# A second pair of gate columns by seven products a block, low parts of five weight tiles by ScalarE and adding transfers, partial sums laid back into PSUM, in a fp32 decoder layer

## The chip, the cores and the metric

One core of a Trainium2 chip. The metric is the device time of one execution in microseconds, lower is better: the median of 3 runs, 1174.49 us (1174.16 to 1174.79). Everything is fp32 in and out. TensorE (PE) multiplies, VectorE (DVE) and ScalarE (ACT) work on tiles in SBUF and PSUM, SyncE (SP) issues plain DMA transfers, GpSimd (POOL) issues the transfers that add to what lies in their target.

## What is computed

One layer over 272 tokens (16 learned ones and 256 of the input) of width 2048. The first half, in which the change lies:

```python
u = rms_norm(h, g_pre_mix[l])
proj = u @ w_in[l]                     # 2048 x 7168: z | v | g | gate_a | gate_b
z_pool, v_conv, g_conv, gate_a, gate_b = jnp.split(proj, splits, axis=-1)
y_a = causal_multiscale_pool(z_pool, w_pool_grp[l], pool_scale[l]) @ w_pool_out[l]
y_b = conformer_conv(v_conv, g_conv, w_dw[l], b_dw[l],
                     conv_ln_g[l], conv_ln_b[l]) @ w_conv_out[l]
m = jax.nn.sigmoid(gate_a) * y_a + jax.nn.sigmoid(gate_b) * y_b
h = h + rms_norm(m @ w_o[l], g_post_mix[l])
```

conformer_conv ends with a LayerNorm over the channels and a silu. The second half, an MLP of width 8192 with a squared ReLU, begins near 490 us of the profile and is the same in both kernels.

## The kernel before

**Products in three parts.** fp32 accuracy is made of fast fp32r products: every operand is split into a rounded part hi and a rest lo, and a product is hi x hi + hi x lo + lo x hi. A weight tile is 1 MB, 128 partitions x 2048. It goes through three steps: SP loads it into a *room* (a raw buffer, L821), ACT casts it to hi (L845), DVE subtracts to get lo (L851). There are three hi and three lo buffers in turn, so the cast of tile n+2 may start no sooner than the product of tile n-1 has ended. Rooms come free as stages end; `loads` (L808) takes the next weight as soon as a room is free for long enough.

**Stages.** Products 0 to 21 are the tiles of w_in for z, v and g (below: Z; 48 matmuls each, L544), product 22 the four matrices of the pooling groups (grp). Beside them DVE does the 31-tap convolution (L981). Then follows an order written out by hand, `MAIN` (L37): p is w_pool_out, a and b are the two gate zones of w_in, c is w_conv_out, o is w_o. A word like `b22` is the weight tile of column block 2 and row block kc 2, in two block products (one for each half of the tokens, t = 0 and 1) of twelve matmuls (L1281). lnm and lnv are the sums for LayerNorm's mean and variance on PE (L1124, L1154), followed on DVE and ACT by the factor, the activations of conv_out with their low part (`s_act`, L1182) and the sums of blocks of them (`forms_c`, L1209). T, CD, OF, fu, k0r, um8, h1 turn, sum or store activations.

**Seven products in place of eight.** `b0P1` to `b0P7` are a 2 x 2 x 2 block: two halves of the tokens, two row blocks, two column blocks (0 and 1). Eight block products become seven, each a sum of activation blocks (a *form*, `forms_u`) with a sum of weight tiles. The products 2, 3 and 4 are the last of their results. After 1, 5, 6 and 7 the bank holds a partial sum that a later product needs in another bank as well: the *give* (`Pair.give`, L1318) copies it out by ACT (L1330), or subtracts it by DVE for 7. `Pair.close` (L1297) adds what was given to the finished bank by DVE (L1303, L1305). The weight sums of products 5, 6, 7 and 4 are made in the room of the first tile: by DVE (L863) where the table `SUMMED` (L44) names the product, otherwise by an adding transfer from POOL (a *bring*, L867). Before, a0, a2, b0, c2 and o0 are such pairs; b's columns 2 and 3 are plain.

**What sets the order.** `Plan` (L48) collects all work of the Z and MAIN stages with its engine and what it reads and writes, gives every piece a time by which it is due (from the row of PE's products, backwards), and writes each engine's instructions in the order in which a list schedule starts them. PE keeps the order of the table. Each engine then runs its own row strictly in order.

Of the kernel before, what the change touches and what calls it, by code (L numbers as in the profile page):

```python
# [18 lines left out]
CW = 512  # L19
# [15 lines left out]
AFTER_G0 = [("z", 0), ("z", 1), ("v", 1), ("z", 2), ("g", 1), ("v", 2), ("g", 2), ("z", 3),  # L35
            ("v", 3), ("g", 3)]
MAIN = (  # L37
# [5 lines left out]
)  # L43
# [168 lines left out]
def hybrid_block(ctx: ExitStack, tc: tile.TileContext, ins: dict, out: bass.AP):  # L212
# [548 lines left out]
    for s in steps:  # L761
        if s[0] == "close":
            index_of[s[1]] = n
        if s[0] == "k1":
            index_of[10] = n
# [6 lines left out]
    index_of[8] = index_of[9] = len(products) - 2  # L772
    uses = []
    for m_, s in enumerate(products):
        if m_ == 0:
            continue
        if s[0] == "S" and s[3] in ADDS:
            onto, what = raw_of(s), block_raw(s, ADDS[s[3]])
            if s[3] in SUMMED.get((s[1], s[2]), "56"):
                uses.append((m_, "sum", [onto, what], None))  # L780
            else:
                uses.append((m_, "bring", [onto], what))
        uses.append((m_, "split", [raw_of(s)], None))
    last_use, to_load = {}, []
    for n, (m_, _, raws_, _) in enumerate(uses):
        for r in raws_:
            if r not in last_use:
                to_load.append(r)
            last_use[r] = n

    rooms = {}
    for r in range(3):
# [12 lines left out]
    early = [2]  # L805
    room_at = {}

    def loads():  # L808
        while to_load:
            r = to_load[0]  # L810
            ends_ = uses[last_use[r]][0]
# [5 lines left out]
            free_rooms.remove(q)  # L817
            src, (rows, _) = source(r)
# [18 lines left out]
    def split_of(m_, q, rows):  # L837
        box, n = split_at[m_], slot0 + m_
        width = CK * CW // (2 if m_ == 1 else 1)
        cuts = [slice(c, c + width) for c in range(0, CK * CW, width)]  # L840

        def high():
            box["flat"] = part_tile("hi", n)
            for cs in cuts:
                nc.scalar.copy(box["flat"][:, cs], rooms[q]()[:, cs])  # L845
            box["hi"] = box["flat"].rearrange("p (k c) -> p k c", k=rows)

        def low():
            lo = part_tile("lo", n)
            for cs in cuts:  # L850
                nc.vector.tensor_sub(lo[:, cs], rooms[q]()[:, cs], f32(box["flat"][:, cs]))  # L851
            box["lo"] = lo.rearrange("p (k c) -> p k c", k=rows)
        return high, low

    def weights(m_):
        while done_uses[0] < len(uses) and uses[done_uses[0]][0] <= m_:
# [8 lines left out]
            elif what == "bring":  # L865
                src, (rows, _) = source(extra)
                plan.add("POOL", 5.38, lambda a=at_rooms[0], src=src, rows=rows: nc.gpsimd.dma_start(  # L867
                    rooms[a]().rearrange("p (k c) -> p k c", k=rows), src, accum_op=ALU.add),
                    reads=names, writes=names)
            else:  # L870
                high, low = split_of(w, at_rooms[0], source(raws_[0])[1][0])
                h_, l_ = half_names(w)
                plan.add("ACT", 1.82, high, reads=names, writes=(h_,), late=0.13)
                plan.add("DVE", 2.22, low, reads=names + [h_], writes=(l_,), late=0.13)
            for r in raws_:
                if last_use[r] == n:
                    free_rooms.append(room_at[r])
# [359 lines left out]
    def finish(stage, t, n, name, src):  # L1237
# [17 lines left out]
        else:  # L1255
# [2 lines left out]
            on_vector(CW, lambda: last_factor(dst(), src(), n), (name, "gmix", dst_name),  # L1258
                      (dst_name,))

    class Pair:


        def __init__(self, stage, n0, whole):
            self.stage, self.n0, self.whole = stage, n0, whole
            self.bank = {}
            self.parts = 1 + (("N", stage, n0 + 1, 2) in products)
            self.gives = {}

        def product(self, t, n, m_, a_, names, gives, last):  # L1270
            key = (t, n)
            opens = key not in self.bank
            if opens:
                self.bank[key] = open_bank()
            bank, ends_ = self.bank[key], bool(gives or last)

            def f():
                box = split_at[m_]
                for k in range(CK):
                    for i, (part, w_) in enumerate(((0, "hi"), (0, "lo"), (1, "hi"))):  # L1280
# [2 lines left out]
                                         stop=ends_ and k == CK - 1 and i == 2,  # L1283
                                         skip_group_check=True)
            on_tensor(2.725, f, half_names(m_) + names, (bank,))
            if gives:
                gives(bank)
            if last:
# [29 lines left out]
        def give(self, s, bank):  # L1318
# [3 lines left out]
                return  # L1322
            t, j = {"1": (0, 0), "5": (1, 1), "6": (0, 1), "7": (1, 1)}[s]
            name, dst = self.place(t, n + j)
            if s == "7":
                on_vector(CW, lambda: nc.vector.tensor_sub(dst(), dst(), banks[bank]),
                          (bank, name), (name,))
# [18 lines left out]
    def counted(stage, t, n):  # L1346
        remaining[stage, t, n] -= 1
        return remaining[stage, t, n] == 0

    def product_n(m_, stage, n, kc):  # L1350
# [12 lines left out]
    def product_s(m_, stage, n0, s, k0):  # L1363
# [10 lines left out]
        row, j = INTO[s]  # L1374
        pair.product(row, n0 + j, m_, a_, waits, (lambda bank: pair.give(s, bank)) if s in "1567"
                     else None, s in "234" and counted(stage, row, n0 + j))

# [53 lines left out]
        loads()  # L1431

    def k1_step():
        free_rooms.remove(10)
        plan.take(names_s[1], ["raw10"])
        plan.take(["raw3", "raw4"], names_y)
        free_rooms.extend((4, 3))
        loads()
# [125 lines left out]
    for s in steps:  # L1564
# [29 lines left out]
        else:  # L1594
            for w in range(m_, min(m_ + 3, len(products))):
                weights(w)
            if m_ >= tail:
                break
            {"Z": product_z, "grp": product_grp, "N": product_n, "S": product_s}[s[0]](m_, *s[1:])
            m_ += 1  # L1600
    for t in range(NT):
# [751 lines left out]
```

## Time and profile before

| | |
|---|---|
| median of 3 runs | 1174.49 us (1174.16 to 1174.79) |
| the profiled execution, its own time | 1174.95 us |
| its span, first to last instruction | 1173.2 us |
| granted TensorE clock | 0.998 |
| moved by DMA | 290.07 MB, mean 247 GB/s |

The profile's first part gives the busy time of each engine with its share of the span; part four follows the chain of work that ended last. PEld is PE's loading of weights, which overlaps its matmuls. A matmul of 128x512 is listed with 0.39 us, yet the next starts 0.23 us later: matmuls are pipelined, and the distance from start to start is what one costs. In rows of a source line the three numbers of a duration are minimum, median and maximum in ns. "DMA to landing" counts from the issue.

### The profile page before, as it was taken

How to read it: one execution, taken by the hardware profiler on the slowest of the kernel's cores; microseconds unless marked ns; L12 is line 12 of the kernel's file. 1: busy time of each engine (PE TensorE's matmuls, PEld its weight loads, DVE VectorE, ACT ScalarE, POOL GpSimd, SP SyncE). 2: the span in 40 equal slices, each digit the busy share in tenths (PEclk: the TensorE clock that was granted, in tenths of full speed). 3: DMA queues.
4: the chain of work that ended last, by engine and by line, in shares of the span. 5: the costliest groups of instructions: out<-in, count | busy, mean ns of one | idle time of the engine just before them, and what ended most of it. 6: DMA issues, size and time to landing. Idle time of an engine off the chain costs nothing.

```text
span 1173.2 us, 15824 instructions
## 1 busy us (share of the span) xinstructions
PE 1161.4 (99%) x6289; PEld 1008.4 (86%) x6289; DVE 1078.6 (92%) x1169; ACT 717.9 (61%) x727; POOL 69.1 (6%) x72
## 2 busy tenths in 40 slices
PE   9999999999999999999999999999999999999997
PEld 8999998788888888898888888888888888888886
DVE  6799999999998998788998998998999989989998
ACT  6634454556478666576775665665656655656655
POOL 1000000000000000000101001000000001010000
PEclk9999999999999999999999999999999999999999
DMA  9955356889866799468999999999999998999955
GB/s 294 285 189 180 108 180 173 248 271 299 218 195 246 209 352 296 150 215 288 261 311 232 248 310 258 243 303 236 282 293 227 327 250 237 329 252 250 327 140 179
DMA packets 188194, 290.07 MB, mean 247 GB/s; under 512 B 4969, under 2 KB 94761, under 8 KB 187336
## 3 DMA queue, kind: packets, MB, share of 16 engines
q1 hardware_dynamic: 161832, 234.31, 58.3%
q0 software_dynamic: 25680, 54.03, 25.2%
q8 instruction: 49, 0.80, 0.3%
q10 hardware_dynamic: 608, 0.73, 0.2%
q14 instruction: 25, 0.20, 0.0%
HBM read 284.85 MB, written 4.19 MB: 246 GB/s over the span
## 4 chain that ended last, share of the span: by engine, by line
PE 98%; DVE 0%; DMA 0%; ACT 0%; issue 0%; ACTq 0%; DVEq 0%
PE bank_u L549 19%; PE bank_k L1281 18%; PE acc_up L2024 13%; PE acc_v L1281 10%; PE bank_u L555 9%; PE bank_k L544 8%; PE bank_a L2024 7%; PE bank_b L2024 6%; PE acc_v L544 4%; PE acc_up L549 1%; PE acc_up L555 1%; PE acc_v L1551 0%; PE bank_k L1551 0%; DMA raw<-in_w_in_dram 0%; PE ht L1616 0%; PE bank_y L1385 0%
## 5 line engine op out<-in xcount | busy, mean ns | idle before, releaser
L549 PE MATMUL bank_u<-m,hi 128*128 128x512 f32 x960 | 329.6, 390 | 0.0
L555 PE MATMUL bank_u<-m,lo 128*128 128x256 f32 x960 | 265.4, 276 | 0.0
L549 PEld LDWEIGHTS bank_u<-m,hi 128*128 128x128 f32 x960 | 180.2, 188 | 37.8
L845 ACT CAST hi<-raw_p 128x2048 fp32r<-128x2048 f32 x70 | 133.8, 1913 | 103.7 <-PE bank_k L1281 28.8
L1854 DVE TENSOR_TENSOR lo<-raw_m,hi 128x2048 fp32r<-128x2048 f32 x79 | 180.8, 2288 | 17.0 <-ACT hi L1849 16.1
L1849 ACT CAST hi<-raw_m 128x2048 fp32r<-128x2048 f32 x79 | 151.1, 1913 | 68.0 <-PE bank_u L549 48.1
L555 PEld LDWEIGHTS bank_u<-m,lo 128*128 128x128 f32 x960 | 180.3, 188 | 1.6
L851 DVE TENSOR_TENSOR lo<-raw_p,hi 128x2048 fp32r<-128x2048 f32 x70 | 159.6, 2284 | 12.7 <-ACT hi L845 12.4
L2024 PE MATMUL acc_up<-hi,forms 128*128 128x512 f32 (+1 forms) x456 | 146.9, 386 | 0.0
L1849 ACT CAST hi<-raw_h 128x2048 fp32r<-128x2048 f32 x42 | 80.3, 1912 | 38.5 <-PE bank_u L549 18.3
L2024 PEld LDWEIGHTS acc_up<-hi,forms 128*128 128x128 f32 x456 | 85.2, 188 | 18.1 <-ACT G L2049 0.2
L1854 DVE TENSOR_TENSOR lo<-raw_h,hi 128x2048 fp32r<-128x2048 f32 x42 | 96.1, 2287 | 5.1 <-ACT hi L1849 4.6
L981 DVE SCALAR_TENSOR_TENSOR c<-a,taps,c 128x256 f32<-128x256 f32 x240 | 100.1, 475 | 0.0
L544 PE MATMUL bank_k<-u_um,hi 128*128 128x272 f32 x512 | 95.2, 287 | 0.0
L1281 PE MATMUL bank_k<-hi,u_um 128*128 128x512 f32 x280 | 88.8, 389 | 0.7 <-ACT sg L1330 0.7
L2024 PE MATMUL acc_up<-lo,forms 128*128 128x512 f32 (+1 forms) x228 | 88.2, 387 | 0.0
L2024 PE MATMUL bank_a<-hi,forms 128*128 128x512 f32 x256 | 84.1, 389 | 0.0
L544 PEld LDWEIGHTS bank_k<-u_um,hi 128*128 128x128 f32 x512 | 79.8, 188 | 0.0
L544 PE MATMUL bank_k<-u_um,lo 128*128 128x272 f32 x256 | 73.3, 287 | 0.0
L1849 ACT CAST hi<-raw_c 128x2048 fp32r<-128x2048 f32 x23 | 43.9, 1908 | 39.1 <-PE bank_u L549 31.5
L2024 PE MATMUL bank_b<-hi,forms 128*128 128x512 f32 x192 | 63.1, 389 | 0.0
L1281 PEld LDWEIGHTS bank_k<-hi,u_um 128*128 128x128 f32 x280 | 52.5, 188 | 12.0 <-ACT sg L1330 1.1
(408 smaller groups left out, 2231.3 us busy)
## 6 DMA issues: line engine op xcount, KB each, us to landing
raw_p<-in_w_in_dram SPq DMA_DIRECT2D x30, 1024.0 KB, 5.6
raw_m<-in_w_down_dram SPq DMA_DIRECT2D x26, 1024.0 KB, 8.7
raw_m<-in_w_down_dram POOLq DMA_DIRECT2D x23, 1024.0 KB, 10.7
raw_h<-in_w_up_dram SPq DMA_DIRECT2D x18, 1024.0 KB, 8.1
raw_h<-in_w_down_dram SPq DMA_DIRECT2D x18, 1024.0 KB, 8.8
raw_m<-in_w_up_dram SPq DMA_DIRECT2D x17, 1024.0 KB, 8.0
raw_k<-in_w_in_dram SPq DMA_DIRECT2D x14, 1024.0 KB, 7.0
raw_a<-in_w_up_dram SPq DMA_DIRECT2D x14, 1024.0 KB, 9.1
```

Of the source, the lines that this page charges most:

```text
L544: nc.tensor.matmul(acc, w[:, k[0], cs], act[:, k[1], a, off:], start=first and n == 0, stop=last and n == 2)
L549: nc.tensor.matmul(acc.rearrange("p (a t) -> p a t", a=2)[:, :, ts], hi[:, k[0], cs], act[:, k[1], :, off + ts.start:off + ts.stop], start ...
L555: nc.tensor.matmul(acc[:, :T], lo[:, k[0], cs], act[:, k[1], 0, off:], start=False, stop=stop, skip_group_check=True)
L845: nc.scalar.copy(box["flat"][:, cs], rooms[q]()[:, cs])
L851: nc.vector.tensor_sub(lo[:, cs], rooms[q]()[:, cs], f32(box["flat"][:, cs]))
L981: nc.vector.scalar_tensor_tensor(C_c()[:, q, :], A_a()[:, q, i:i + T], taps[:, q, i:i + 1], C_c()[:, q, :], op0=ALU.mult, op1=ALU.add)
L1281: nc.tensor.matmul(banks[bank], a_(k, part), box[w_][:, k, :], start=opens and k == 0 and i == 0, stop=ends_ and k == CK - 1 and i == 2, s ...
L1849: nc.scalar.copy(box["flat"], raw_in(room))
L1854: nc.vector.tensor_sub(lo, raw_in(room), f32(box["flat"]))
L2024: nc.tensor.matmul(acc, forms[h][:, f, k, a_, :], box[w_][:, k, cs], start=start and k == 0 and n == 0, stop=stop and k == KH - 1 and n == ...
```

## The change

Five parts, all in the mix stage:

1. Columns 2 and 3 of the second gate, row blocks 0 and 1 (`b20 b21 b30 b31`), become `b2P1` to `b2P7`. `MAIN` is written anew around them, and `SUMMED` divides the sums between DVE and POOL anew.
2. `LOW_BY_DMA` names five early tiles (13, 14, 16, 18 of Z and 22, the pooling groups) whose low part isn't made by DVE: ACT writes the negated rounded tile into another room (L823), an adding transfer of POOL adds the raw weight from memory to it (L827), and ACT copies the result to lo (L883).
3. `LAY_BEHIND`: where a bank opens two products or more behind the give that its result needs, ACT copies the partial sum into the bank (`lay`, L1314), and the matmuls add to it; DVE's addition at the end is left out.
4. A plain product right behind a give into a bank that it uses itself begins with its other half of the tokens (`given`).
5. Room 10 is ready for weights at the first gate product rather than at k1.

```diff
-    "p20 p30 p01 p21 p00 p11 fu p10 p31 k1 a0P1 a2P1 a2P2 a0P5 a13 a12 a0P6 a0P3 a0P7 a02 a0P4 "
-    "a2P5 a03 a32 a33 a2P6 a2P3 a2P7 a22 a2P4 a0P2 b0P1 a23 b22 b21 b33 b23 b0P5 b32 lnm b0P6 b20 "
-    "b0P7 b31 lnv b0P4 b12 b0P3 k0r b02 b13 b0P2 b30 b03 um8 c01 c2P1 c11 c10 T10 c2P5 c2P6 c2P3 "
...
+    "p00 fu p31 p01 a0P1 p30 p21 p20 p10 p11 k1 a2P2 a0P5 a13 a0P6 a0P3 a2P1 a0P7 a12 a0P4 "
+    "a2P5 a33 a03 a2P6 a32 a2P7 a02 a2P4 a0P2 a2P3 a23 a22 b2P1 b2P5 b33 b2P2 b2P6 b2P3 b2P7 "
+    "b0P1 b23 b2P4 b32 b0P5 b0P2 lnm b22 b12 b0P6 b0P3 lnv b0P7 b02 b0P4 b03 b13 k0r um8 c2P1 "
+    "c00 c2P5 c11 c01 c10 T00 T01 c2P2 c2P6 T10 c2P3 c2P7 o20 c2P4 T11 CD o31 T21 T30 o30 T20 "
+    "T31 o21 o22 OF o0P1 o0P5 h1 o23 o0P3 o0P6 o12 o0P7 o02 o13 o0P4 o03 o0P2 o32 o33 "
-SUMMED = {('gate0', 0): '67', ('gate0', 2): '57', ('gate1', 0): '6', ('co', 2): '456', ('o', 0): '67'}
+SUMMED = {('gate0', 0): '67', ('gate0', 2): '56', ('gate1', 0): '5', ('co', 2): '6', ('o', 0): '57', ('gate1', 2): '56'}
+LOW_BY_DMA = "13 14 16 18 22"
+LAY_BEHIND = 2
...
+    def low_by_dma(m_, q):
+        low_at[m_] = q
+        raw = raw_of(products[m_])
+        src, (rows, _) = source(raw)
+
+        def minus_high(a=room_at[raw]):
+            nc.scalar.activation(rooms[q]().bitcast(F32R), rooms[a](), AF.Copy, scale=-1.0)
+
+        def add_raw():
+            whole = rooms[q]().rearrange("p (k c) -> p k c", k=rows)
+            nc.gpsimd.dma_start(whole, src, accum_op=ALU.add)
...
-            for cs in cuts:
+            for cs in cuts if m_ not in low_at else ():
                 nc.vector.tensor_sub(lo[:, cs], rooms[q]()[:, cs], f32(box["flat"][:, cs]))
+            if m_ in low_at:
+                nc.scalar.copy(lo, rooms[low_at[m_]]())
...
+        def lay(self, t, n, bank):
+
+            name, dst = self.place(t, n)
+            self.laid.add((t, n))
+            on_scalar(CW, lambda: nc.scalar.copy(banks[bank], dst()), (name,), (bank,))
...
             if opens:
                 self.bank[key] = open_bank()
+                if made[0] - self.held.get(key, made[0]) >= LAY_BEHIND:
+                    self.lay(t, n, self.bank[key])
             bank, ends_ = self.bank[key], bool(gives or last)
+            opens = opens and key not in self.laid
...
-            if self.whole or (t, n) == (1, self.n0):
+            if self.whole or (t, n) == (1, self.n0) or (t, n) in self.laid:
                 finish(self.stage, t, n, bank, src)
...
-        order_ = range(NT)
+        order_ = reversed(range(NT)) if given == [(stage, 0, n)] else range(NT)
+        given.clear()
```

**PE where a0P5 is followed by a13.** Names behind the arrow are weight part and activations; `u_um` is the first slice of a row block and `u_um_156` the other three, `forms_u` the sum for product 5; `bank_k_...` and `acc_v_...` are PSUM banks. Before:

```order
L1281 MATMUL bank_k_400<-lo_2268,forms_u 128x512
L1281 MATMUL bank_k_400<-hi_2249,forms_u 128x512
L1281 MATMUL bank_k_400<-hi_2270,u_um 128x512
L1281 MATMUL bank_k_400<-lo_2273,u_um 128x512
...
L1281 MATMUL bank_k_401<-hi_2270,u_um 128x512
L1281 MATMUL bank_k_401<-lo_2273,u_um 128x512
```

and with the change:

```order
L1330 MATMUL acc_v_1_165<-lo_2259,forms_u 128x512
L1330 MATMUL acc_v_1_165<-hi_2238,forms_u 128x512
L1330 MATMUL bank_k_399<-hi_2278,u_um 128x512
L1330 MATMUL bank_k_399<-lo_2283,u_um 128x512
...
L1330 MATMUL acc_v_1_165<-hi_2278,u_um 128x512
L1330 MATMUL acc_v_1_165<-lo_2283,u_um 128x512
```

a13 went on in the bank that a0P5 had just filled and that is copied out at this point; now its twelve matmuls for the other half of the tokens stand in between, in a bank of their own.

**ACT in the Z stage, tiles 15 to 18**, with the change. hi_1308, hi_1372, hi_1437 and hi_1502 are the casts of tiles 15, 16, 17 and 18; the two L823 are the negated copies of 16 and 18, lo_1443 the low part of 16.

```order
L875 CAST hi_1308<-raw_s0a 128x2048
L823 ACTIVATE raw_p_405<-raw_p_406 128x2048
L823 ACTIVATE raw_s0a<-raw_p_407 128x2048
L875 CAST hi_1372<-raw_p_406 128x2048
L875 CAST hi_1437<-raw_s0a 128x2048
L883 CAST lo_1443<-raw_p_405 128x2048
L1004 ACTIVATE g_666<-g_666 128x272
L875 CAST hi_1502<-raw_p_407 128x2048
```

Before, the four casts follow each other with nothing but convolution work between; now the negated copies stand right behind tile 15's cast, and the low part of tile 16 is read on ACT behind the cast of tile 17, in the place of a subtraction on DVE.

**ACT in the gate stage around b0P2**, with the change. hi_2964, hi_3000, hi_3019, hi_3050 and hi_3073 are the casts of b32, b0P5, b0P2, b22 and b12, which is the order of the products; `sg_2088` holds the partial sums and acc_v_0_164 is the bank of b0P2.

```order
L875 CAST hi_2964<-raw_p_405 128x2048
L1382 COPY sg_2088<-bank_k_402 128x512
L875 CAST hi_3000<-raw_p_406 128x2048
L875 CAST hi_3019<-raw_k_2276 128x2048
L875 CAST hi_3050<-raw_k_2276 128x2048
L1314 COPY acc_v_0_164<-sg_2088 128x512
L1277 ACTIVATE sg_2088<-sg_2088,r_in 128x512
L875 CAST hi_3073<-raw_p_405 128x2048
```

The L1314 copy, which b0P2's matmuls wait for, stands behind the cast of b22, the product after b0P2; before there was no such copy, and DVE added the partial sum after the bank was finished.

More of the change, by code (lines that the diff above doesn't have):

```diff
@@ L772, in hybrid_block @@
     index_of[8] = index_of[9] = len(products) - 2
+    first_gate = index_of[10] = next(m_ for m_, s in enumerate(products)
+                                     if s[0] in "NS" and s[1][:4] == "gate")
     uses = []
@@ L789, in hybrid_block @@
             last_use[r] = n
+        if what == "split" and m_ in lows:
+            to_load.append(("lo", m_))
     rooms = {}
@@ L806, in hybrid_block @@
     room_at = {}
+    low_at, planned = {}, set()
+    def low_by_dma(m_, q):
[7 more added lines that the diff above has]
+            nc.gpsimd.dma_start(whole, src, accum_op=ALU.add)
+        plan.add("ACT", 1.82, minus_high, reads=(f"raw{room_at[raw]}",), writes=(f"raw{q}",),
+                 late=0.13)
+        plan.add("POOL", 5.38, add_raw, reads=(f"raw{q}",), writes=(f"raw{q}",))
     def loads():
@@ L870, in weights @@
             else:
+                planned.add(w)
                 high, low = split_of(w, at_rooms[0], source(raws_[0])[1][0])
@@ L873, in weights @@
                 plan.add("ACT", 1.82, high, reads=names, writes=(h_,), late=0.13)
-                plan.add("DVE", 2.22, low, reads=names + [h_], writes=(l_,), late=0.13)
+                if w in low_at:
+                    plan.add("ACT", 1.82, low, reads=(f"raw{low_at[w]}",), writes=(l_,), late=0.13)
+                    free_rooms.append(low_at[w])
+                else:
+                    plan.add("DVE", 2.22, low, reads=names + [h_], writes=(l_,), late=0.13)
             for r in raws_:
@@ L1259, in finish @@
                       (dst_name,))
+    made = [0]
     class Pair:
@@ L1374, in product_s @@
         row, j = INTO[s]
+        given[:] = [(stage, row, n0 + j)] if s in "1567" else []
         pair.product(row, n0 + j, m_, a_, waits, (lambda bank: pair.give(s, bank)) if s in "1567"
```

25 lines of the change are left out of this document (19 added, 6 removed), and 2 rows, old and new, of the table MAIN.

## The prediction

> **What bounds the kernel now.** I read the page's engine totals and chain first, then all of PE's waits.
>
> ```profile
> PE 1161.4 (99%) x6289; PEld 1008.4 (86%) x6289; DVE 1078.6 (92%) x1169; ACT 717.9 (61%) x727; POOL 69.1 (6%) x72
> PE 98%; DVE 0%; DMA 0%; ACT 0%; issue 0%; ACTq 0%; DVEq 0%
> PE acc_v L602 <- ACT u_um L515: 1.4, 1, 1.4
> PE idle L458 <- POOL ident masks.py:199: 1.4, 1, 1.4
> PE bank_k L1281 <- ACT sg L1330: 0.7, 1, 0.7
> ```
>
> The last three rows are every wait of PE over the whole span (us in total, times, longest): the first two lie in the first ten microseconds, the third is one stall in the gate stage. PE is the chain. So the time falls by what PE no longer does, and rises by each microsecond for which PE finds a weight part, a form or a bank late. DVE is the engine behind it; the table by stage (PE, PEld, DVE, ACT, POOL busy; clock; DMA share; GB/s) shows how near.
>
> ```profile
> 60.00:155.00 95.00, 95.00 (x772) 95.00 (x771) 94.75 (x155) 36.61 (x28) 0.00 (x0) 1.00 0.49 156
> 155.00:204.00 49.00, 49.00 (x241) 41.57 (x240) 49.00 (x82) 27.55 (x31) 1.37 (x1) 1.00 0.60 184
> 204.00:375.00 171.00, 170.32 (x751) 140.39 (x750) 165.04 (x174) 109.17 (x92) 7.68 (x6) 1.00 0.81 244
> 375.00:490.00 115.00, 115.00 (x524) 95.20 (x523) 104.41 (x88) 70.64 (x70) 5.15 (x5) 1.00 0.79 253
> ```
>
> The stages are Z (weights of w_in), pool, gates, and conv_out with w_o. DVE is full in Z and pool and keeps 6 us free in the gates, yet PE never waits for it: it is a tie, so work taken from DVE earns nothing by itself, and work delayed on DVE would cost at once.
>
> **What the change removes.** Columns 2 and 3 of the second gate, rows kc 0 and 1, were eight block products of twelve matmuls (b20, b21, b30, b31) and become seven (b2P1 to b2P7). The chain in order of time has eight such block products in one piece:
>
> ```profile
> 289.90 21.76 PE bank_k L1281 x96
> ```
>
> 21.76 / 96 = 0.227 us a matmul, at clock 1.00 by the table. Everything else on PE is moved, not changed: 6284 matmuls become 6272. Gain: 12 x 0.227 = **2.72 us**, all on PE's path.
>
> The stall goes too. It lies where a0P5's bank is copied out (a give) while a13 opens in that same bank:
>
> ```profile
> 214.96 0.39 PE L1281 MATMUL bank_k<-hi,forms_u 128*128 128x512 f32 x1
> 215.39 0.59 ACT L1330 COPY sg<-bank_k 128x512 f32<-128x512 f32 x1 [0.65 <-PE bank_k L1281]
> 216.02 0.50 PE L1281 MATMUL bank_k<-hi,u_um 128*128 128x512 f32 x1 [0.68 <-ACT sg L1330]
> ```
>
> Start to start is 216.02 - 214.96 = 1.06 us in place of 0.23, so 0.83 us are lost. By the order, a13 now begins with its other token half in another bank, and comes back to the given bank 12 matmuls, 2.72 us, later; the copy takes 0.59. Nothing else waits there, so **0.83 us** go. The other gives have a different bank or a plain product behind them already, or PE's waits would show them.
>
> Sum against the profiled execution (1174.95, of which the span is 1173.2): 1174.95 - 2.72 - 0.83 = 1171.40. That execution lies 0.46 above the median of 1174.49, so on the medians **1170.94**.
>
> **What it adds, and what hides it.** The durations:
>
> ```profile
> L845 ACT CAST hi<-raw_p 128x2048 fp32r<-128x2048 f32 x70 | 133.8, 1913 | 103.7 <-PE bank_k L1281 28.8
> L851 DVE TENSOR_TENSOR lo<-raw_p,hi 128x2048 fp32r<-128x2048 f32 x70 | 159.6, 2284 | 12.7 <-ACT hi L845 12.4
> L863 DVE TENSOR_TENSOR raw_p<-raw_p,raw_p x6: 2277/2284/2286, 217.1 to 439.5; 128x2048 f32<-128x2048 f32 x6
> L1330 ACT COPY sg<-acc_v x7: 579/582/583, 209.0 to 325.5; 128x512 f32<-128x512 f32 x7
> L1305 DVE TENSOR_TENSOR sg<-sg,bank_k x6: 673/676/680, 227.5 to 372.3; 128x512 f32<-128x512 f32 x6
> ```
>
> DVE: three more tiles to split (105 for 102) and five low parts taken off, so two low parts fewer, 4.57 us; as many sums of weight tiles as before; with an addition of 0.68 less, some 5 us less in all. Most of it, five times 2.28 = 11.4 us, is taken out of the Z stage, where DVE has nothing free. It is worth nothing alone (PE doesn't wait there); it pays for the closer spacing of the gate tiles, which each need a low part, and so is a cover for the 2.72.
>
> ACT: three more casts, five negated parts, five copies of low parts (13 x 1.91 = 24.8 us, taking the negation and the copy like a cast of the same shape), five lays and three more gives at 0.58: about 29 us, on an engine that is busy 36.6 of 95 us in Z. Its total does not matter; its order does, at two places.
>
> *The lay at b0P2.* The rows of ScalarE in the gate stage show it: the cast for b22 (hi_3050) can start only when b32's product frees that buffer, which is when b0P5 starts, 2.72 us ahead of b0P2. Cast and lay take 1.91 + 0.58 = 2.49. Some 0.2 us are left, so this costs nothing, or up to 0.3 with the hand-overs of about 0.04 at each end that the stall above shows. The other four lays have over 3 us.
>
> *Tile 16's low part.* Its steps follow each other: cast of tile 15, negated copy, adding transfer, cast of tile 17, copy to lo.
>
> ```profile
> 101.84 1.91 ACT L845 CAST hi<-raw_p 128x2048 fp32r<-128x2048 f32 x1
> 113.69 1.91 ACT L845 CAST hi<-raw_s0a 128x2048 fp32r<-128x2048 f32 x1 [4.00 <-PE bank_k L544]
> 119.65 11.84 PE acc_v L544 x96
> ```
>
> The first row is tile 15's cast, the second tile 17's, the third begins with tile 16's product. The negated copy ends at 101.84 + 2 x 1.91 = 105.7, so a transfer that takes L lands at 105.7 + L, its copy ends 1.91 later, and PE waits beyond L = 12.0 us.
>
> No adding transfer with 1 KB rows ran before; the nearest are those with 2 KB rows, of the same 1 MB:
>
> ```profile
> L867 POOL DMA_DIRECT2D raw_p<-in_w_in_dram x6: 1276/1280/1367, 198.3 to 316.3; - x6
> DMA to landing us min/median/max: 8.3/9.3/10.5
> raw_p<-in_w_in_dram SPq DMA_DIRECT2D x30, 1024.0 KB, 5.6
> q1 hardware_dynamic: 161832, 234.31, 58.3%
> q0 software_dynamic: 25680, 54.03, 25.2%
> ```
>
> Lower end: like these rows, L = 8.3 to 10.5 and nothing lost. In the Z stage plain loads with 1 KB rows (128x8x256 in the order) ran at 156 / 0.49 = 318 GB/s of full share, against 234.31 MB / (0.583 x 1173.2 us) = 343 for the SP queue as a whole, so short rows hardly cost the plain kind. Upper end: if the adding kind pays for each row, twice the median, 18.6, which stalls 6.6 us. I take the lower end, being 1 KB rows of an unsaturated stage (share 0.49), and keep the upper for the range.
>
> The Trainium skill, "DMA: Bandwidth & Descriptors", section "Anatomy of one DMA — SWDGE (gpsimd) path", fits such a transfer as 2.0 us plus its bytes by 436 GB/s, an estimate of 4.4 us for 1 MB whatever its rows. The trace has 8.3 to 10.5 from issue to landing, so the row decides; by the page there would be no late transfer at all and 1170.9 would stand.
>
> **Brings that come nearer.** Two more weight sums of w_in and two of w_conv_out come by adding transfers in place of DVE. Each must fit between the last reading of its room and its own cast. The tightest of before stood beside a0P5:
>
> ```profile
> 198.30 1.37 POOL L867 DMA_DIRECT2D raw_p<-in_w_in_dram  x1 [159.46 <-DVE lo L851]
> 212.47 0.39 PE L1281 MATMUL bank_k<-hi,forms_u 128*128 128x512 f32 x1
> ```
>
> From issue to product 14.2 us, for landing, cast and low part (1.91 + 2.28 = 4.2): 10.0 left for the landing. a0P5 stands three block products behind the reader that frees its room (a0P1, a2P1, a2P2). In the new order c2P5 stands as many behind c2P1 (c2P1, and c00's two), so 10.0 against 8.3 to 10.5: 0 to 0.5 us. o0P6 stands four behind o0P5, whose sum on DVE lies in between: 10.0 + 2.72 - 2.28 = 10.4, 0 to 0.1. Where DVE reaches the freeing instruction late, by half of one of 2.28, each costs 1.1 more. I take 0.2 for both, with the landing at its median and little lateness. The gates and conv_out carry 2 MB more each, at shares of 0.81 and 0.79 of the engines.
>
> **LayerNorm nearer to its reader.** lnv, the sums of squares on PE, was 13 block products ahead of the first product of conv_out (c01) and is now 8 ahead of it (c2P1), by the order of the program: 8 x 2.72 = 21.8 us.
>
> ```profile
> 336.45 0.38 PE L1154 MATMUL bank_y<-sq,ones 128*128 128x256 f32 x1
> 357.91 1.22 DVE L1182 TENSOR_TENSOR s_act<-c,s_act 128x1024 fp32r<-128x1024 f32 x1
> ```
>
> Before, the first half of conv_out's activations ended 357.91 + 1.22 - 336.45 = 22.7 us after lnv, among other DVE work, and its reader came 35 us after lnv. If none of that moves behind, c2P1 waits 0.9; if it does, nothing. I take 0.1, since the order puts these steps ahead of weights that are needed later.
>
> Together 0.3 us for small new waits, so the forecast is **1171.3 us**.
>
> **Rivals.**
> *Part is given back.* Late brings at c2P5 and o0P6 (0.6, and 2.3 where DVE is late for both), LayerNorm (0.9) and the lay (0.3) add up to 4.1 at most: up to 1175.0, middle 1173.0. For it: each lies within a microsecond of its row. Against: PE's only stall of before is none of these kinds, though a0P5's bring stood as close.
> *Slower.* Adding transfers with 1 KB rows take twice as long. Then tile 16 waits 6.6 us, and the transfers for 18 and 22 queue behind it: 1170.9 + 6.6 = 1177.5. It costs from L = 12.0 on, and makes the kernel slower than measurable from L = 18, where 5.9 us are lost. For it: the adding queue moves 54.03 MB / (0.252 x 1173.2) = 183 GB/s of full share where the plain one moves 343, so adding does cost engine time. Against: that is already in the 8.3 to 10.5.
> *It doesn't do what it says.* The twelve matmuls are gone by the order, but the stall could stay if PE meets the copy elsewhere: 1174.49 - 2.72 = 1171.8, still faster.
>
> **How the numbers follow.** Forecast, with the stall kept or not: 0.63, from 1170.4 (the sum less 0.5, most of the 0.63 between the slowest and the fastest run) to 1172.1. Part given back, up to 1175.0: 0.25. Slower mechanism: 0.12, of which 0.04 ends within 0.2%. A measurement of this kernel tells 0.2%, 2.35 us, from no change, so faster is below 1172.14. Faster: 0.63 and a little of the second case, 0.66; same: 0.26; slower: 0.08. The range goes from 1170.4 to 1175.0 and leaves out the slower mechanism.
>
> **What would show it.** The matmul line of the seven products at 0.227 a matmul, no wait of PE on a give, and PE's waits still short: right. A wait of PE on a Z weight's low part: the transfers are slow, and their time to landing is the test. A wait at c2P1 for s_act, at c2P5 or o0P6 for a low part, at b0P2 for the lay: the second case, each by its own row. DVE still full in Z would say that the five low parts were not its load. The prediction is wrong if PE's clock moves from 1.00 or if such waits pass 1.2 us together.

## The result and the profile after

The changed kernel takes **1182.86 us** (median; 1182.48 to 1183.98) against 1174.64 in the same runs of the kernel before: a ratio of 1.0072 (95% interval 1.0054 to 1.0089), 0.7% slower. The forecast was 1171.3, at most 1175.0. The profiled execution after is one of 1183.98, with a span of 1182.2, 9.0 us longer than the one of before.

The page's engine totals and its chain that ended last, after:

```profile
PE 1164.0 (98%) x6277; PEld 1009.5 (85%) x6277; DVE 1074.2 (91%) x1166; ACT 745.0 (63%) x748; POOL 81.9 (7%) x81
PE 80%; issue 7%; DVE 6%; DMA 5%; ACT 2%; SPq 0%; POOL 0%; DVEq 0%; ACTq 0%; POOLq 0%
```

The twelve matmuls are gone (6289 to 6277 on PE) and DVE has 4.4 us less to do, where some 5 were forecast. But PE holds only 80% of the chain, where it held 98%. All of PE's waits, in total, times, longest:

```profile
PE ht L1673 <- issue: 3.1, 1, 3.1
PE acc_v L546 <- ACT lo L883: 1.9, 1, 1.9
PE idle L460 <- POOL ident masks.py:199: 1.4, 1, 1.4
PE bank_k L546 <- DVE g L1002: 1.3, 1, 1.3
PE acc_v L546 <- DVE y L1139: 1.0, 1, 1.0
PE bank_k L1330 <- DVE sg L1378: 0.7, 1, 0.7
PE acc_v L604 <- ACT u_um L517: 0.5, 1, 0.5
PE mt_in L507 <- DMA m_wide<-in_meta_dram: 0.2, 1, 0.2
```

The wait on ACT's copy of a give has gone. New are tile 16's low part (1.9), the banks around the pooling groups (1.3 and 1.0), a give that DVE subtracts at b0P7 (0.7), and 3.1 us at the start of the MLP, where the first transposes (`ht`) come late: 8.0 us. Behind two of these places PE also runs slowly. Busy times by stretch (PE, PEld, DVE, ACT, POOL; the column behind them is PE's granted clock):

```profile
121.30:125.00 3.70, 3.66 (x29) 3.67 (x30) 3.70 (x11) 2.98 (x4) 0.00 (x0) 1.00 1.17 238
165.00:169.00 4.00, 4.00 (x15) 3.41 (x14) 4.00 (x7) 3.46 (x6) 0.00 (x0) 0.58 0.10 6
507.20:511.30 4.10, 4.07 (x13) 3.41 (x14) 2.32 (x6) 2.19 (x7) 0.58 (x1) 0.50 0.51 195
511.30:516.00 4.70, 4.70 (x36) 4.70 (x35) 3.21 (x12) 2.86 (x12) 0.58 (x1) 0.81 0.16 59
```

Behind tile 16's wait the clock stays at 1.00; behind the two waits at the groups it is 0.58 for 4 us, 1.7 us lost, and behind the 3.1 us at the MLP 0.50 for 4.1 us and 0.81 for 4.7 more, 2.05 + 0.9 lost. So 8.0 + 4.65 are new; 2.7 (matmuls), 0.8 (the old stall) and 0.9 (`L604`, 1.4 before) are saved. That makes 8.2 of the 9.0; the rest is too short for the list of waits and stays unassigned. By place, Z and pool lost 5.9, the start of the MLP 6.0 and b0P7 0.7.

The stages, with the same columns as before:

```profile
60.00:155.00 95.00, 93.05 (x755) 92.84 (x754) 86.85 (x163) 51.86 (x36) 7.82 (x5) 1.00 0.80 196
155.00:204.00 49.00, 46.61 (x227) 39.38 (x226) 48.89 (x80) 28.54 (x34) 1.28 (x1) 0.97 0.67 201
204.00:375.00 171.00, 170.31 (x750) 140.28 (x749) 167.17 (x161) 111.21 (x90) 11.56 (x9) 1.00 0.88 254
```

In Z DVE was busy 94.75 us of 95 and is now 86.85, though PE waits for DVE soon after. So it stood idle while work was due. What it waited for, by the timeline of ACT and of DVE (start, us, instruction, idle time before it and what ended it):

```profile
104.10 1.91 ACT L883 CAST lo<-raw_s0a 128x2048 fp32r<-128x2048 f32 x1 [6.34 <-DMA raw_s0a<-in_w_in_dram]
105.91 0.60 ACT L1011 ACTIVATE c<-a,vecs,taps 128x256 f32<-128x256 f32 x1
106.54 0.48 DVE L1018 SCALAR_TENSOR_TENSOR c<-a,taps,c 128x256 f32<-128x256 f32 x1 [4.87 <-ACT c L1011]
```

ACT's copy of tile 14's low part stands 6.34 us in ACT's row until the adding transfer has landed. Behind it stands the first tap of a convolution block (L1011), and behind that DVE's other taps: DVE idles 4.87 us here, and once more behind tile 18's copy. The five adding transfers (L827):

```profile
DMA to landing us min/median/max: 8.9/12.8/14.9
```

The quickest took 8.9 us, so 1 KB rows by themselves need not cost; three of the five took 12.8 to 14.9, above the 8.3 to 10.5 of before. The slowest, tile 14's, was issued within 9 us of three plain loads. That crowding made it slow fits, but was not tried by itself.

The other large loss lies at the end of w_o, where the first w_up weights are split. After, on ACT and DVE:

```profile
492.62 1.90 ACT L875 CAST hi<-raw_p 128x2048 fp32r<-128x2048 f32 x1
494.56 2.29 DVE L881 TENSOR_TENSOR lo<-raw_p,hi 128x2048 fp32r<-128x2048 f32 x1 [0.85 <-ACT hi L875]
502.59 1.91 ACT L360 CAST parts<-raw 128x2048 fp32r<-128x2048 f32 x1 [3.54 <-DMA raw<-in_w_up_dram]
504.40 0.59 ACT L1581 ACTIVATE ng_offset=None)_3_0_4173<-bank_k 128x512 f32<-128x512 f32 x1
```

and before:

```profile
485.13 1.91 ACT L845 CAST hi<-raw_p 128x2048 fp32r<-128x2048 f32 x1 [2.15 <-PE acc_v L1281]
487.07 2.29 DVE L851 TENSOR_TENSOR lo<-raw_p,hi 128x2048 fp32r<-128x2048 f32 x1 [2.00 <-ACT hi L845]
494.68 1.92 ACT L358 CAST parts<-raw 128x2048 fp32r<-128x2048 f32 x1 [1.36 <-DMA raw<-in_w_up_dram]
496.50 0.59 ACT L1527 ACTIVATE ng_offset=None)_3_0_4152<-bank_k 128x512 f32<-128x512 f32 x1
```

The first row is the cast of the last w_o tile, o33. Its low part frees the room of the third w_up tile; that tile's cast waits for its load, and behind it in ACT's row stand the squares for the RMSNorm whose result PE must transpose. The cast of o33 moved by 7.5 us, though PE is only some 4 us later there. It may start when the product three tiles back has ended, and the product just ahead of the last two tiles is now o0P2, 2.7 us long, where it was o31 with 5.4.

### The profile page after: what moved, and what is told of

Same layout as the page of the kernel before. It is cut to its first block, busy times and chain, and to the rows that moved or that the text cites. A ratio compares the mean times of both kernels' runs of the same rounds, so it can differ in the third digit from the quotient of the medians.

```text
span 1182.2 us, 15846 instructions
## 1 busy us (share of the span) xinstructions
PE 1164.0 (98%) x6277; PEld 1009.5 (85%) x6277; DVE 1074.2 (91%) x1166; ACT 745.0 (63%) x748; POOL 81.9 (7%) x81
## 4 chain that ended last, share of the span: by engine, by line
PE 80%; issue 7%; DVE 6%; DMA 5%; ACT 2%; SPq 0%; POOL 0%; DVEq 0%; ACTq 0%; POOLq 0%
PE bank_u L551 18%; PE bank_k L1330 14%; PE acc_up L2081 13%; PE bank_u L557 9%; PE bank_a L2081 7%; PE acc_v L1330 6%; PE bank_b L2081 6%; DMA raw_p<-in_w_in_dram 3%; DVE lo L881 3%; PE acc_up L551 1%; DMA raw_s0a<-in_w_in_dram 1%; DVE c L1018 1%; PE acc_v L546 1%; PE bank_k L546 1%; ACT hi L875 1%
## 5 line engine op out<-in xcount | busy, mean ns | idle before, releaser
L1911 DVE TENSOR_TENSOR lo<-raw_m,hi 128x2048 fp32r<-128x2048 f32 x79 | 180.8, 2289 | 16.9 <-ACT hi L1906 15.9
L1906 ACT CAST hi<-raw_m 128x2048 fp32r<-128x2048 f32 x79 | 151.1, 1912 | 67.8 <-PE bank_u L551 47.8
L875 ACT CAST hi<-raw_p 128x2048 fp32r<-128x2048 f32 x71 | 135.4, 1911 | 72.0 <-PE bank_k L1330 23.8
L881 DVE TENSOR_TENSOR lo<-raw_p,hi 128x2048 fp32r<-128x2048 f32 x66 | 150.6, 2286 | 18.6 <-ACT hi L875 14.3
L1330 PE MATMUL bank_k<-hi,u_um 128*128 128x512 f32 x216 | 69.6, 391 | 0.7 <-DVE sg L1378 0.7
L1911 DVE TENSOR_TENSOR lo<-raw_c,hi 128x2048 fp32r<-128x2048 f32 x23 | 52.6, 2287 | 8.9 <-ACT hi L1906 8.9
```

Of the source, the lines that this page charges most:

```text
L1330: nc.tensor.matmul(banks[bank], a_(k, part), box[w_][:, k, :], start=opens and k == 0 and i == 0, stop=ends_ and k == CK - 1 and i == 2, s ...
L1906: nc.scalar.copy(box["flat"], raw_in(room))
L1911: nc.vector.tensor_sub(lo, raw_in(room), f32(box["flat"]))
```

## The experiments

Each time is a median with its ratio to the kernel before, run beside it.

**The losses one by one.** Low parts by DVE again, everything else as changed:

```diff
-LOW_BY_DMA = "13 14 16 18 22"
+LOW_BY_DMA = ""
```

> The changed kernel with no low part made by ScalarE and adding transfers (all by VectorE again). Theory: these transfers are the loss in the Z stage. ScalarE stood 6.3 us behind one of them, VectorE's convolution then waited 4.9 us for ScalarE, and PE lost 2.0 us at tile 16 and 4.5 us around the pooling groups (stalls and the slower clock after them). Without them both go: 1182.9 - 6.5 = 1176.4 us, and the 5 us at the start of the MLP stay. Rival: VectorE needs the 11.4 us that the change takes from it in Z, since the forms of the gates now come earlier; then PE waits for low parts or for banks in Z and pool instead, and the time is 1182 us or more.

1191.59 us (1.0151; 1.0137 to 1.0165): slower, and by far. PE's longest waits:

```profile
PE bank_y L1161 <- DVE v L1149: 12.6, 1, 12.6
PE ht L1673 <- issue: 2.8, 1, 2.8
PE bank_k L1330 <- DVE lo L881: 2.2, 2, 1.8
```

No wait in Z is left, but PE stands 12.6 us at lnm until DVE has finished the convolution. So the rival's reason held, at a later place than it named (lnm, not Z and pool). The relief of DVE was not a convenience: the new order needs it.

The end of w_o:

```diff
-... o0P4 o03 o0P2 o32 o33
+... o0P4 o0P2 o03 o32 o33
```

> The changed kernel with o0P2 ahead of o03 in place of behind it, nothing else. Theory: the 3.1 us stall of PE at the start of the MLP and the slow clock behind it (5.1 us in all) come from the cast of o33, which may start only when the product three tiles back has ended; with the single product o0P2 just ahead of the last two tiles this is 2.7 us before them in place of 5.4, so the third w_up load, its cast on ScalarE and the squares behind it are all late. The swap gives 1182.9 - 5 = 1177.8 us, with the losses in Z unchanged. Rival: the w_up loads are late since two more adding transfers and the earlier delay crowd the queues; then nothing changes: 1182.9 us with the same wait.

1178.76 us (1.0040; 1.0028 to 1.0052), 4.1 less than the change, and the wait of `ht` is gone from the list. The step is shown: o33's cast starts at 489.2 in place of 492.6. Both edits together:

> The changed kernel with both edits: no low part by adding transfers, and o0P2 ahead of o03. Theory: the two losses are apart and add up: 1182.9 - 6.5 - 5 = 1171.4 us, about what twelve matmuls and the one stall less should give, with 0.9 us left at b0P7. Rival: VectorE without the relief is late in the gates, 1175 us or more.

1186.72 us (1.0111; 1.0097 to 1.0125): the swap gives 4.9 us here too, and the rest is the rival: PE waits 12.7 us for the means.

The part of the change that was to remove the stall at a0P5, put into the kernel before:

```diff
-        order_ = range(NT)
+        order_ = reversed(range(NT)) if given == [(stage, 0, n)] else range(NT)
+        given.clear()
```

> The kernel before with one part of the change alone: a plain product right behind a give into its own bank begins with its other half of the tokens. Theory: the stall of 0.83 us at a0P5 goes and nothing else moves: 0.8 us less than before (0.07%). Rival: the copy is met by PE in another place, or the order of the banks makes a new wait: no difference, with a wait of PE on a give in the list.

1174.18 us (0.9999; 0.9990 to 1.0008): no difference that these runs can tell, though 0.83 us, 0.07%, would lie inside the interval. The trace decides: the stall is gone from the list, and in its place stands

```profile
PE acc_v L1281 <- DVE lo L851: 1.0, 1, 1.0
```

PE comes sooner and waits for a low part 25 us further on, until 240.7 us. In the kernel before DVE ends that low part at the same time, 240.6, and PE doesn't wait for it.

**Other ways to hand over the low parts**, all with the swap at the end of w_o, so to be held against its 1178.76. GpSimd makes the last copy (the planner's entry for it is changed with it), so that ACT's row is free:

```diff
-                nc.scalar.copy(lo, rooms[low_at[m_]]())
+                nc.gpsimd.tensor_copy(lo, rooms[low_at[m_]]())
```

> The changed kernel with o0P2 ahead of o03, and the last copy of the five early low parts made by GpSimd in place of ScalarE. Theory: VectorE is the bound up to LayerNorm's means (it idles 0.6 us there before, 9.0 in the run with the swap alone), and it idles because ScalarE's queue stands behind copies that wait for adding transfers. With the copies on another queue 6.4 us of the idle time go, and with them the waits of PE around the pooling groups (3.6 us) and at VectorE's late low part (1 us): 1178.8 - 4.6 = 1174.2 us, or 1172.5 if tile 16 is in time too. Rival: the transfers themselves are too late, whoever copies; then PE waits for GpSimd's copies in place of ScalarE's and the time stays at 1178 us or rises by a slow copy.

1179.07 us (1.0037; 1.0023 to 1.0051). DVE's waits on ACT in Z are all gone, so the link from ACT's row to DVE's idle time is shown; the time stays. GpSimd's copies, by their source line (minimum, median, maximum in ns):

```profile
L883 POOL CAST lo<-raw_p x3: 2489/3483/5237, 89.9 to 152.4; 128x2048 fp32r<-128x2048 f32 x3
L883 POOL CAST lo<-raw_s0a x2: 2015/3240/4464, 101.8 to 126.4; 128x2048 fp32r<-128x2048 f32 x2
```

a DVE instruction that ran four times, once beside such a copy:

```profile
L1087 DVE TENSOR_TENSOR d<-dm,d x4: 692/698/2409, 56.6 to 150.6; 128x512 fp32r<-128x512 f32 x4
```

and the taps between 60 and 160 us, with GpSimd's copies

```profile
L1018 DVE SCALAR_TENSOR_TENSOR c<-a,taps,c x115: 469/481/2126, 61.3 to 160.0; 128x256 f32<-128x256 f32 x115
```

and with ACT's, in the run with the swap alone:

```profile
L1018 DVE SCALAR_TENSOR_TENSOR c<-a,taps,c x114: 463/472/486, 61.0 to 159.9; 128x256 f32<-128x256 f32 x114
```

The instruction of 0.69 us took 2.41, and a few taps up to 2.13, while the median tap kept its length. All taps together were busy for 54.8 us in place of 47.8. The 6.4 us that DVE no longer waited for ACT it lost to a few long instructions.

The same without tile 16's transfer, and ACT's copies without it:

```diff
-LOW_BY_DMA = "13 14 16 18 22"
+LOW_BY_DMA = "13 14 18 22"
```

> As the run with GpSimd's copies, but tile 16 has its low part by VectorE again (four tiles by adding transfers). Theory: the wait of PE at tile 16 is gone and VectorE's 2.3 us more are covered by the idle time that it no longer has: 1172.5 us, below the kernel before. Rival: VectorE, the bound up to the means, is late by these 2.3 us at LayerNorm's means: 1174.5 us or more, with a wait of PE on the means.

> The changed kernel with o0P2 ahead of o03 and without tile 16 among the low parts by adding transfers; ScalarE copies the other four as in the change. Theory: PE's wait at tile 16 (1.7 us) goes, but ScalarE still stands behind the copy for tile 14 and VectorE behind ScalarE (4.6 us idle), so the waits around the groups stay in part: 1176.5 us. Rival: the collision of the two transfers for tiles 16 and 18 was the whole loss; then all waits in Z go and the time is 1173 us.

With GpSimd 1180.43 us (1.0050; 1.0031 to 1.0068): PE now waits 2.0 us on GpSimd's copy of another tile and 2.9 us on DVE's low parts, neither the theory's 1172.5 nor the rival's wait at the means. With ACT 1177.56 (1.0028; 1.0018 to 1.0038): tile 16's wait is gone and the waits at the groups stay (1.8 and 0.5), as that run's theory had it. DVE idles 4.3 us behind ACT, but behind two casts (L875), no longer behind a tap.

The planner was then given a longer price for the adding transfer, so that ACT's copies stand later in its row:

```diff
-        plan.add("POOL", 5.38, add_raw, reads=(f"raw{q}",), writes=(f"raw{q}",))
+        plan.add("POOL", 9.0, add_raw, reads=(f"raw{q}",), writes=(f"raw{q}",))
```

> The changed kernel with o0P2 ahead of o03, and the adding transfers of the low parts priced at 9.0 in place of 5.38 in the planner's table, so that ScalarE's copies stand later in its row, behind the convolution's first taps, and the negated copies earlier. Theory: the loss in Z is ScalarE's row, not the transfers themselves: VectorE's idle time up to LayerNorm's means falls from 9.0 us to under 3, the waits of PE at tile 16 and the groups go (5.3 us), and the time is 1173.5 us. Rival: the transfers (8.9 to 14.9 us to landing) are too long for these tiles in any row; PE then waits for a low part in Z and the time stays at 1178 us.

> As the run with the price of 9.0, without tile 16 among the five. Theory: no two adding transfers collide, VectorE has 2.3 us more to do but no longer idles: no wait of PE in Z, and 1172.5 us if VectorE reaches LayerNorm's means in time, 1174 if it is late by its 2.3 us. Rival: as with five tiles, the time stays near 1177.6, where four tiles with the old price stood.

Five tiles: 1188.55 us (1.0112; 1.0096 to 1.0127), four: 1181.61 (1.0058; 1.0045 to 1.0070). Both worse than the old price. With five, the transfers landed after 9.0 to 16.7 us, and

```profile
PE acc_v L546 <- ACT lo L883: 7.7, 1, 7.7
```

shows tile 16 later than ever: its copy stands behind tile 17's cast in ACT's row, and that cast waits for its plain load. The load was issued at 107.7 us, only 1.7 later than in the change, but took 14.3 us in place of 5.2: two adding transfers, issued at 106.2 and 109.8, ran beside it and took 11.6 and 16.7. The rival's wait came, though the time is 10 us above its 1178: at these places the transfers are too long, in either order.

No partial sums laid into PSUM:

```diff
-LAY_BEHIND = 2
+LAY_BEHIND = 1000
```

> The changed kernel with o0P2 ahead of o03 and no partial sum laid into PSUM (VectorE adds all of them at the end, as before). Theory: lays take five additions of 0.68 us, 3.4 us, from VectorE, of which two lie ahead of LayerNorm's means; VectorE being the bound there, the time rises by 1 to 2 us, to 1180.3 us. Rival: PE waits for other things in Z and VectorE has slack behind the means, so nothing changes: 1178.8 us.

1178.74 us (1.0037; 1.0024 to 1.0049): no difference from 1178.76, as the rival had it. The lays neither cost nor earn anything that these runs can tell.

**Which engine sets the time.** Four of the convolution's 30 taps on DVE left out, in the changed kernel with the swap and without adding transfers for low parts, and in the kernel before. Both then leave out part of the convolution; they are for the time alone.

```diff
-        for i in range(1 + moved, TAPS):
+        for i in range(1 + moved, TAPS - 4):
```

> The changed kernel with o0P2 ahead of o03 and no low parts by adding transfers (1186.7 us), and with the last four taps of the convolution left out: 32 instructions of VectorE fewer, 32 x 0.396 = 12.7 us. Theory: VectorE is the bound up to LayerNorm's means, where PE stood 12.6 us; with the same time taken from VectorE all of it goes and PE's gain shows: 1174.4 - 2.7 - 0.8 = 1170.9 us, with no wait of PE over 0.5 us after the start. Rival: PE waits in the gates for other reasons as well (casts, brings, the give at b0P7): 1174 us or more.

> The kernel before with the same four taps left out. Theory: VectorE is tied with PE there and not above it, so 12.7 us less on VectorE are worth nothing to PE: 1174.4 us, and VectorE idles 12 us more up to the means. Rival: VectorE already holds PE back in ways that the list of waits doesn't show, and the time falls by 1 us or more.

1171.40 us (0.9985; 0.9974 to 0.9996) and 1174.87 (1.0003; 0.9993 to 1.0012): the theory's 1170.9 and 1174.4 within 0.5 us each. All that PE waits for in the first:

```profile
PE idle L460 <- POOL ident masks.py:199: 1.4, 1, 1.4
PE bank_u L551 <- DVE F_raw L1986: 0.3, 1, 0.3
PE acc_v L604 <- ACT u_um L517: 0.2, 1, 0.2
PE acc_up L551 <- DVE q_mix L1565: 0.2, 1, 0.2
```

and, by their source lines, DVE's means and PE's lnm there (behind the durations stand the first and the last start):

```profile
L1149 DVE TENSOR_TENSOR v<-v,c x6: 409/418/419, 298.1 to 318.1; 128x256 f32<-128x256 f32 x6
L1161 PE MATMUL bank_y<-v,ones x2: 377/378/378, 330.4 to 330.6; 128*128 128x256 f32 x2
```

With 12.7 us taken from DVE for nothing, the new order is 2.9 us faster than the kernel before (0.5 to 3.1 by the interval), and no wait of PE over 0.3 us is left behind the start. Without them, by the run with no low parts, the last of the means starts at 345.0 us and lnm 0.5 behind. In the kernel before it is nearly a tie: the last of the means starts at 316.8, lnm at 319.7, and 12.7 us less on DVE earn nothing.

Two ways to give relief with less waiting:

```diff
-LOW_BY_DMA = "13 14 16 18 22"
+LOW_BY_DMA = "13"
...
-MOVED_TAPS = {}
+MOVED_TAPS = {0: 4, 1: 4, 2: 4, 3: 4}
```

The first line stands in the order and the sums of before, with the other half of the tokens first and no partial sums laid; the second in the changed kernel with the swap and no low parts by transfers.

> The table of the kernel before, with the other half of the tokens first behind a give (1174.2 us alone: the stall went, and a wait of 1.0 us for a low part of VectorE came), and the low part of tile 13 alone by an adding transfer, the one of the five that nobody waited for. Theory: 2.3 us less on VectorE cover the 1.0 us: 1173.4 us. Rival: the new wait stays, or ScalarE's two more steps cost VectorE as much as they give: 1174.2 us.

> The changed kernel with o0P2 ahead of o03, no low parts by adding transfers, and 16 pairs of taps made by ScalarE and added by transfers of 256 KB from SBUF to SBUF instead of VectorE (32 instructions, 12.7 us). Theory: if these small transfers land in time, VectorE has the relief that it needs, PE waits nowhere for long, and the time is 1171.5 us, below the kernel before. Rival: VectorE's taps of the same channels stand behind the chain of four transfers, it idles as it did behind ScalarE, and the time is 1178 us or more.

1175.62 us (1.0012; 1.0003 to 1.0021): the wait of 1.0 stays, now 1.2, so it is not DVE's total that makes it. The low part that PE waits for stands behind a weight sum in DVE's row (L863, here L895). In the kernel before, in the run with the other half first and here, that sum starts at 236.1, 236.1 and 236.2 us, each time as the load of its second tile lands: issued at 226.8, 226.7 and 226.9, it took 9.2 to 9.4 us. Less work on DVE did not bring that load forward. And 1186.26 (1.0106; 1.0092 to 1.0119), with these waits of DVE up to the means:

```profile
DVE c L1018 <- DMA c<-z: 6.2, 2, 3.1
DVE lo L881 <- ACT hi L875: 7.0, 5, 2.0
```

DVE stands behind the small transfers as it stood behind ACT, as that run's rival had it.

Last, relief from the weight sums, brought by adding transfers, with tile 13's low part alone (`LOW_BY_DMA = "13"`). The diff is that of the first of two runs; the second keeps the sum of a2P6 on DVE and adds tile 22:

```diff
-SUMMED = {('gate0', 0): '67', ('gate0', 2): '56', ('gate1', 0): '5', ..., ('gate1', 2): '56'}
+SUMMED = {('gate0', 0): '6', ('gate0', 2): '5', ('gate1', 0): '', ..., ('gate1', 2): '5'}
```

> The changed kernel with o0P2 ahead of o03, only tile 13's low part by an adding transfer, and four weight sums of the gates (a0P7, a2P6, b2P6, b0P5) brought by adding transfers in place of VectorE: 5 x 2.28 = 11.4 us less for VectorE up to LayerNorm's means, as much as the five low parts gave, without ScalarE's row in the way. Theory: no waits in Z, VectorE just in time at the means: 1172.5 us, below the kernel before. Rival: four more megabytes of adding transfers at a share of 0.83 to 0.88 come too late for their casts; PE waits for low parts behind them in the gates: 1176 us or more.

> As the run with four more brings, but with three (a0P7, b2P6, b0P5) and the low parts of tiles 13 and 22 by adding transfers: again 11.4 us. Theory: 1172.5 us, as there. Rival: the copy for tile 22 holds up ScalarE behind its transfer at the end of Z, where PE then waits for banks around the pooling groups, 1175 us or more.

1198.40 (1.0201; 1.0184 to 1.0218) and 1199.06 us (1.0207; 1.0192 to 1.0222). The rival held in the first; the second is as late, but not at the groups where its rival had it. In both PE waits for casts and low parts behind late transfers in the gates, in the first

```profile
PE acc_v L1330 <- DVE lo L881: 5.6, 3, 2.2
PE bank_k L1330 <- ACT hi L875: 3.8, 1, 3.8
PE bank_k L1330 <- DVE lo L881: 3.6, 1, 3.6
```

with transfers of up to 16.9 us. No version that computes the whole layer beat the kernel before.

## Why the prediction was wrong, step by step

- **"PE is the chain."** True of the trace, and not enough. PE's list of waits shows who came last, not by how little: DVE, busy 94.75 of 95 us in Z and 49 of 49 in the pool stage, finished the means 2.5 us ahead of lnm (316.8 + 0.4 against 319.7). The prediction called it a tie, and then counted PE's gain in full.
- **The cover failed, and this is the first of the two steps on which the sum fell.** The prediction took the 11.4 us off DVE in Z as "a cover for the 2.72". It counted three more tiles to split over the whole mix stage, but not how many of them DVE must split ahead of lnm. Four plain tiles make eight block products; in the block of seven, each product has a tile of its own. By the end of the means, from 60 us on, DVE had done these low parts (L851, L881) and weight sums (L863, L895), first in the kernel before, then in the run with no low parts by transfers (busy us and, in brackets, the number):

```profile
60.00:317.30 257.30, 121.43 (x55) 1.00 0.69 209
60.00:317.30 257.30, 11.42 (x5) 1.00 0.69 209
60.00:345.50 285.50, 139.98 (x62) 0.98 0.69 207
60.00:345.50 285.50, 15.95 (x7) 0.98 0.69 207
```

Nine more steps of 2.28 us are 20.5 us more work (the busy time counts what neighbours overlap only once), while lnm itself stands only four block products, 10.7 us, later (330.4 in the run with fewer taps against 319.7). Without the 11.4 us PE stood 12.6 us at lnm, so they were needed whole. They did not come whole: ACT's row decided them, and DVE idled 6.6 us behind a tap of ACT and 1.5 more behind a cast, as its waits in Z show:

```profile
DVE c L1018 <- ACT c L1011: 6.6, 2, 4.9
DVE lo L881 <- ACT hi L875: 1.5, 1, 1.5
```

In the changed kernel this cost 5.9 us in Z and pool; without the low parts by transfers these waits are gone and the 12.6 us at lnm stand in their place.
- **"Its total does not matter; its order does, at two places."** At a third: tile 14's copy ahead of L1011. The prediction followed what PE needs from ACT, and not what DVE needs from it.
- **The start of the MLP, the second step, is a term that the sum put at nothing.** "Everything else on PE is moved, not changed" was read as if the end of the stage were untouched. The stall and the slow clock behind it took 6.0 us of the profiled execution; the swap of two words gave 4.1 us of the medians back.
- **The 2.72 us** are consistent with the run with fewer taps, 1171.40, which is 2.9 us below the kernel before. That it lies so near to 1171.3 is partly luck: the interval is 2.6 us wide, and that kernel leaves out taps and has another end of w_o.
- **The 0.83 us** were not to be had: "Nothing else waits there" holds for that place and overlooked a low part 25 us further on, for which PE now waits 1.0.
- **Tile 16** was named as the place of the slower rival, with the point from which it decides, L = 12.0. Its transfer took only 8.9 us and PE waited all the same, since its negated copy came at 108.2 in place of 103.8: ACT stood behind tile 14's copy, whose transfer took 14.9. So the place was right and the mechanism wrong by a link, and the range of 8.3 to 10.5 for a transfer held for two of the five.
- **The give at b0P7** was ruled out by "The other gives have a different bank or a plain product behind them already": it is one that DVE makes, behind a low part that waits for a bring of 8.3 us. It cost 0.7.
- **LayerNorm, lay and brings at c2P5 and o0P6** cost nothing that the list of waits shows.
- **The price of a stall** was taken as its length. The slow clock behind two places cost 1.7 us on top of 2.3 and 2.95 on top of 3.1.

## What to carry to other kernels

When the engine behind the bound is busy nearly all of a stage, count its work up to each point where the bound must meet it, for the old order and the new: a step taken from the bound is worth only what that second engine keeps up with. Relief that goes through another engine's row and a transfer is worth its time less the idle time of whoever stands behind it in that row. And look at the last instructions of a reordered stage: what frees a room there starts the next stage's loads.

## What was not expected of the hardware

A wait of PE of 3.1 us was followed by 4.1 us at a clock of 0.50, and waits of 1.3 and 1.0 within 3.3 us by 4 us at 0.58, while a single one of 1.9 was followed by 1.00. The pair doesn't always cost this: in the run with the swap PE waited 1.3 and 1.0 us at the same place, and the clock behind them was

```profile
165.00:170.00 5.00, 5.00 (x26) 4.20 (x26) 5.00 (x9) 5.00 (x10) 0.00 (x0) 1.00 0.30 75
```

So the 1.7 us lost there differ from one execution to the next. The Trainium skill, "TensorE: Matmul & The Clock Gate", section "What's actually happening", has the clock fall to half after an idle window of about 3.4 us that runs free of the kernel. Here both times PE waited for less than that, 3.1 us in one piece and 2.3 in two, so a window need not be idle throughout; a window that runs free would fit the difference between the two runs, but no run here shows where it lies.

GpSimd's cast of 128x2048 took 2.0 to 5.2 us and made a DVE instruction of 0.69 us take 2.41. The Trainium skill, "SBUF — State Buffer", section "SBUF: two separate sides", says that GpSimd and a DVE instruction with two inputs in SBUF lock each other out for a whole instruction; the trace agrees, with that instruction of two inputs, which ended 0.55 us behind the end of the cast (95.67 against 95.12).

Adding transfers of 1 MB took 8.2 to 17.6 us from issue to landing over all these runs. Beside two of them a plain load took 14.3 us in place of 5.2, so they slow others too; what makes the long ones long was not tried by itself.
